# Start addresses of the stationary tiles in a macaron mLSTM and S5 layer on one Trainium2 core

## The chip, the core and the metric

The kernel runs on one core of one Trainium2 chip. The core has a matrix engine (TensorE, in the tables PE, and PEld for its weight loads), a vector engine (DVE), a scalar engine (ACT), a general engine (POOL) and a queue for transfers (SP). The metric is the device time of one execution in microseconds, lower is better. A matmul on TensorE takes two operands from the on-chip memory (SBUF): the stationary one, 128 x 128, which a weight load brings into the array, and the moving one, up to 512 columns, which then streams past it. In this text "spacing" is the time from the start of one matmul to the start of the next.

## What is computed

One decoder layer on 256 tokens of width 2048, all in float32: a SwiGLU block, a mixer with four mLSTM heads beside 64 groups of an S5 state space, and a second SwiGLU block, each behind an RMS norm.

```python
x = x + 0.5 * swiglu(rms_norm(x, ffn1_norm), ffn1_w1, ffn1_w3, ffn1_w2)   # D_FF = 5632
h = rms_norm(x, mix_norm)
proj = h @ w_in                       # q|k, v, o, i, f of the mLSTM, u of the S5 part
hm = rms_norm(mlstm_chunkwise(...)) * sigmoid(o)
y = gelu(real(scan(S5)) + d_skip * u); hs = y * sigmoid(y @ w_glu + b_glu)
x = x + concat(hm, hs) @ w_out
x = x + 0.5 * swiglu(rms_norm(x, ffn2_norm), ffn2_w1, ffn2_w3, ffn2_w2)
out = rms_norm(x, final_norm)
```

## The kernel before

The weights are read from HBM once. `plan` lists all weight steps; each step is two 128-row slices of one matrix and up to 512 columns. `fetch` loads a step into `wraw` over the SP queue (4 buffers), ACT copies it into `whi` (rounded to the matmul's 32-bit format, 3 buffers), and DVE takes the rest, `wlo = wraw - whi` (3 buffers). Activations are split in the same way into a high and a low part, so one product of the reference is three matmuls: high by high, low by high, high by low.

`step_tok` (line 175) is the main loop, for all products whose result lies with tokens on the partitions. The stationary operand is a 128 x 128 block of an activation, the moving one a row of `whi` or `wlo`, 512 columns wide (344 for the third of `w_in` that holds the output gates, OGW). A step is twelve matmuls: for each of the two slices (kk = 0 and 1) and each of two token halves one with the high and one with the low activation against `whi`, then four against `wlo`. Its stationary tiles are, by stage:

- `xh`, `xl` (four tiles each, 128 x 4 x 256): the transposed x, made by `transpose_x`;
- `gh`, `gl`: the gated products of a SwiGLU, made by `split_T`;
- `hmh`, `hml` and `hsh`, `hsl`: the outputs of the mLSTM heads and of the S5 part, before `w_out`.

`gemm_ch` (lines 223, 224, 229) makes the products whose result lies with channels on the partitions (u, q, k, and the S5 gate). There the roles are exchanged: 128-column blocks of `whi` and `wlo` are stationary, and `xh`, `xl` or `yh`, `yl` move, 256 columns at a time. `tail_mm` (lines 477 to 479) makes the last quarter of the last product with 256 moving columns.

Everything on SBUF comes from pools of tiles. The pools lie one behind the other along a partition in the order in which `setup`, `ffn` and `mixer` open them, and the tiles of a pool in the order in which they are first asked for, each rounded up to 32 bytes. So the length of an early tile sets where all later ones begin. In the order of their places: constants, `x`, `xh`/`xl`, `wraw`, `whi`, `wlo`, small tiles, `junk`, the S5 tiles (`s5k0`, `s5rot`, `s5w1`, `s5w2`), and then the pools of a stage, which begin with `gh`/`gl` in the SwiGLU blocks and with `uT`, `u4`, `yT`, `yh`, `yl` and the tiles that `hmh`, `hml`, `hsh`, `hsl` share in the mixer. `WIDE` is the width of the four tiles `qkp0`, `qkp1`, `vx0` and `vx1`; `hmh` and `hml` are put into the same places later.

The order of work on each engine is the program's own, with matters that fill gaps (the S5 parameters in the first block, the S5 groups in the mixer) spread over the weight steps by `tick`. Names on the rows below: `accb` and `tpb` are PSUM banks, `tpb<-ident,s` is a transposition on TensorE of the gated products (the identity moves, `s` is stationary), `tpb<-u,w1x` a product of the S5 part in plain float32, `u<-uT` the transfer that rearranges the S5 input inside SBUF, `s5rot<-spillrot` the load of an S5 table that the first block had written to HBM.

Of the kernel before, what the change touches and what calls it, by code (L numbers as in the profile page):

```python
# [8 lines left out]
F32 = mybir.dt.float32  # L9
F32R = mybir.dt.float32r  # L10
# [6 lines left out]
P = 128  # L17
S = 256
TT = S // P
# [3 lines left out]
NC = 512  # L23
# [12 lines left out]
EPS = 1e-6  # L36
S5_RATE = 0.62
AHEAD = 2
WIDE = 1152
WARM = 7  # L40
MAGIC = 12582912.0
LOG2E = 1.4426950408889634
# [18 lines left out]
class _Layer:  # L61
# [174 lines left out]
    def setup(self):  # L236
        nc = self.nc
        self.const = self.pool("const")
        self.xp = self.pool("xp")
        self.xTp = self.pool("xTp")  # L240
        self.wraw = self.pool("wrawp", 4)
        self.whi = self.pool("whip", 3)
        self.wlo = self.pool("wlop", 3)
        self.small = self.pool("small", 2)
        self.junkp = self.pool("junkp", 1)
        self.s5p = self.pool("s5p", 2)
        self.dram = self.ctx.enter_context(self.tc.tile_pool(name="s5dram", bufs=1, space=DRAM))
        self.acc = self.ctx.enter_context(self.tc.tile_pool(name="acc", bufs=4, space=PSUM))
        self.tp = self.ctx.enter_context(self.tc.tile_pool(name="tp", bufs=4, space=PSUM))
        c = self.const  # L250
        self.x = [self.xp.tile([P, TT, NC], F32, name=f"x{i}") for i in range(4)]
        xin = self.a["x"][0].rearrange("(t p) n -> p t n", p=P)
        vec0 = self.s5p.tile([KD, P], F32, name="vec0", tag="s5k0")
        nc.sync.dma_start(out=vec0, in_=self.a["ffn1_norm"][0].rearrange("(k p) -> k p", p=P))
        self.load_x = lambda i, a=0, b=NC: nc.sync.dma_start(out=self.x[i][:, :, a:b],
                                                             in_=xin[:, :, i * NC + a:i * NC + b])
        idle = self.junkp.tile([P, NC + 112], F32, name="junk")[:, :NC]
        nc.vector.memset(idle, 0.0)
        self.idle = idle.bitcast(mybir.dt.bfloat16)[:, :NC]
        self.warm(WARM)  # L260
        self.ident = c.tile([P, P], F32, name="ident")
        make_identity(nc, self.ident)
        self.ones = c.tile([P, P], F32, name="ones")
        nc.vector.memset(self.ones, 1.0)
        nc.scalar.activation(self.ones[:, 0:1], self.ones[:, 0:1], AF.Square)
        self.mhalf = c.tile([P, 72], F32, name="mhalf")[:, :8]
        nc.vector.memset(self.mhalf, -0.5)
        self.cols0 = c.tile([P, KD], F32, name="cols0")
        b = self.bank()
        nc.tensor.transpose(b[:, :KD], vec0, self.ident[:KD, :KD])  # L270
        nc.vector.tensor_copy(self.cols0, b[:, :KD])
        rows = 16 + 16 + 32 + 8 * 4
        vecs = self.s5p.tile([rows, P], F32, name="vecs", tag="s5k0")
        r = 0
        where = {}
        for name, n in (("mix_norm", 16), ("ffn2_norm", 16), ("conv_w", 32), ("conv_b", 8), ("mlstm_norm", 8),
                        ("d_skip", 8), ("b_glu", 8)):
            src = self.a[name][0]
            if name == "conv_w":
                src = src.rearrange("w (j p) -> (w j) p", p=P)  # L280
            elif name == "d_skip":
                src = src.rearrange("(j r) h -> j (r h)", r=8)
            else:
                src = src.rearrange("(k p) -> k p", p=P)
            nc.gpsimd.dma_start(out=vecs[r:r + n, :], in_=src)
            where[name] = r
            r += n
        self.cols = c.tile([P, rows], F32, name="cols")

        def late():  # L290
            b = self.bank()
            nc.tensor.transpose(b[:, :rows], vecs, self.ident[:rows, :rows])
            nc.vector.tensor_copy(self.cols, b[:, :rows])
            w = where["b_glu"]
            nc.vector.tensor_scalar(self.cols[:, w:w + 8], self.cols[:, w:w + 8], 0.5, None, op0=ALU.mult)
            w = where["mlstm_norm"]
            nc.vector.tensor_scalar(self.cols[:, w:w + 8], self.cols[:, w:w + 8], 0.5, None, op0=ALU.mult)
        self.after(6, late)
        self.col = lambda name, i: self.cols[:, where[name] + i:where[name] + i + 1]
        gb = c.tile([P, 2, H], F32, name="gb")  # L300
        nc.gpsimd.dma_start(out=gb[:, 0, :], in_=self.a["b_i"][0].partition_broadcast(P))
        nc.gpsimd.dma_start(out=gb[:, 1, :], in_=self.a["b_f"][0].partition_broadcast(P))
        self.gb = gb
# [22 lines left out]
    def transpose_x(self, c, gain, halves=(0, 1)):  # L326
        nc = self.nc
        if halves[0] == 0:
            self.xh[c] = self.xTp.tile([P, 4, S], F32R, name=f"xh{c}")
            self.xl[c] = self.xTp.tile([P, 4, S], F32R, name=f"xl{c}")  # L330
        xh, xl = self.xh[c], self.xl[c]
        for half in halves:
            b = self.bank()
            for i in range(2):
                kt = half * 2 + i
                for t in range(TT):
                    o = i * S + t * P
                    nc.tensor.transpose(b[:, o:o + P], self.x[c][:, t, kt * P:(kt + 1) * P], self.ident)  # L338
            for i in range(2):
                kt = half * 2 + i  # L340
                g = gain(c * 4 + kt)
                src = b[:, i * S:(i + 1) * S]
                nc.scalar.activation(xh[:, kt, :], src, AF.Copy, scale=g)
            for i in range(2):
                kt = half * 2 + i
                g = gain(c * 4 + kt)
                src = b[:, i * S:(i + 1) * S]
                nc.vector.scalar_tensor_tensor(xl[:, kt, :], src, g, xh[:, kt, :].bitcast(F32),
                                               op0=ALU.mult, op1=ALU.subtract)
# [417 lines left out]
        self.ffn1_rate = n_tasks / (n_steps - 8)  # L767

    def s5_tiles(self, skip=None):
        return [self.s5p.tile([P, w], F32, name=f"s5{nm}") if i != skip else None for i, (nm, w) in  # L770
                enumerate((("rot", 1024), ("w1", 512), ("w2", 512), ("k0", 128)))]


    def mixer(self, chunk_done):
# [4 lines left out]
        with ExitStack() as ctx:  # L779
# [181 lines left out]
            for hf in range(2):  # L961
                acc = self.pair()
                self.gemm_ch(acc, self.xs, win, KD, QK0 + hf * NC)
                qkp[hf] = ma.tile([P, WIDE], F32, name=f"qkp{hf}", tag=f"qkp{hf}")[:, :4 * (S + 3)].rearrange("p (j s) -> p j s", j=4)
                G.memset(qkp[hf][:, :, 0:3], 0.0)
# [60 lines left out]
            for c in range(2):  # L1026
                v = ma.tile([P, WIDE], F32, name=f"vx{c}", tag=f"vx{c}")[:, :4 * (DV + 1)].rearrange("p (t h d) -> p t h d", t=TT, h=2)
                G.memset(v[:, :, :, DV:], 1.0)
# [201 lines left out]
```

## Time and profile before

| what | value |
|---|---|
| median of three runs | 1861.88 us (1860.5 to 1862.27) |
| the profiled execution | 1860.78 us |
| its span, first to last instruction | 1859.1 us |
| TensorE busy with matmuls | 1826.6 us, 98% of the span |
| DVE, ACT, POOL busy | 1072.0, 817.7, 346.6 us |
| mean granted clock of TensorE | 0.993 of full speed |

The profiled execution took 1.7 us more than its span, and lies 1.1 us under the median. A busy TensorE is not one at its peak: the records of matmuls overlap, since each is drawn with the time that it needs to run through. So the spacing of the starts is what says how fast the stream goes.

### The profile page before, as it was taken

The numbers are of one execution on the slowest core, as the hardware profiler recorded it, in microseconds if no ns is written. First come the engines' busy times: TensorE is split into PE (matmuls) and PEld (weight loads), VectorE is DVE, ScalarE is ACT, GpSimd is POOL, SyncE is SP. The second block draws the span as 40 slices with busy tenths as digits, with TensorE's granted clock in tenths as the row PEclk, the third lists the DMA queues.
The fourth block names the chain that finished last, engine by engine and source line by source line (L and its number), as shares of the span: only waits on it lengthen the run. The fifth ranks groups of instructions, "written<-read, shape, count | busy, mean of one in ns | idle before, by whom it ended". The sixth has DMA issues, their size and how long they took to land.

```text
span 1859.1 us, 24158 instructions
## 1 busy us (share of the span) xinstructions
PE 1826.6 (98%) x9221; PEld 1541.4 (83%) x9221; DVE 1072.0 (58%) x1287; ACT 817.7 (44%) x977; POOL 346.6 (19%) x525
## 2 busy tenths in 40 slices
PE   9999999999999999997999999999999999999998
PEld 7888888888888888986978888888888888888887
DVE  5457866555555555587888765545554444455454
ACT  6444444344444445433544464444443334444443
POOL 3000999900000000175324200000000000000011
PEclk9999999999999999998999999999999999999999
DMA  8666676676666665876766556666665566666554
GB/s 264 192 192 181 194 219 210 220 228 204 191 197 200 185 197 194 206 167 180 156 172 178 177 183 213 191 186 190 190 190 192 194 194 187 191 192 191 188 195 141
DMA packets 191252, 358.27 MB, mean 193 GB/s; under 512 B 12320, under 2 KB 29344, under 8 KB 191008
## 3 DMA queue, kind: packets, MB, share of 16 engines
q1 hardware_dynamic: 186992, 344.58, 63.3%
q0 software_dynamic: 4000, 11.10, 1.6%
q8 instruction: 72, 1.18, 0.3%
q10 hardware_dynamic: 144, 1.05, 0.1%
q14 instruction: 44, 0.36, 0.1%
HBM read 344.62 MB, written 11.01 MB: 191 GB/s over the span
## 4 chain that ended last, share of the span: by engine, by line
PE 93%; DVE 3%; DMA 1%; issue 1%; ACT 0%; POOL 0%; SPq 0%; ACTq 0%; DVEq 0%; POOLq 0%
PE accb L175 83%; PE accb L223 2%; PE accb L224 2%; PE accb L229 2%; DVE wlo L157 1%; PE tpb L489 1%; DMA wraw<-in_w_in_dram 1%; DVE A L869 1%; PE tpb L338 1%; PE tpb L854 0%; PE accb L479 0%; PE accb L478 0%; PE accb L477 0%; DMA u<-uT 0%; PE tpb L893 0%
## 5 line engine op out<-in xcount | busy, mean ns | idle before, releaser
L157 DVE TENSOR_TENSOR wlo<-wraw,whi 128x1024 fp32r<-128x1024 f32 (+1 forms) x630 | 789.9, 1256 | 691.5 <-ACT whi L155 689.3
L155 ACT CAST whi<-wraw 128x1024 fp32r<-128x1024 f32 (+1 forms) x630 | 656.5, 1043 | 926.3 <-PE accb L175 817.5
L175 PE MATMUL accb<-whi,xh 128*128 128x512 f32 (+1 forms) x1568 | 610.1, 389 | 5.9 <-ACT whi L155 5.9
L175 PE MATMUL accb<-whi,xl 128*128 128x512 f32 (+1 forms) x1568 | 605.6, 386 | 0.0
L175 PE MATMUL accb<-wlo,xh 128*128 128x512 f32 (+1 forms) x1568 | 414.7, 386 | 6.8 <-DVE wlo L157 6.8
L175 PEld LDWEIGHTS accb<-whi,xh 128*128 128x128 f32 x1568 | 295.6, 189 | 64.8 <-ACT whi L155 7.2
L175 PEld LDWEIGHTS accb<-wlo,xh 128*128 128x128 f32 x1568 | 293.2, 189 | 66.7 <-DVE wlo L157 8.9
L175 PEld LDWEIGHTS accb<-whi,xl 128*128 128x128 f32 x1568 | 296.0, 189 | 56.5
L175 PE MATMUL accb<-whi,gh 128*128 128x512 f32 x664 | 259.8, 391 | 0.0
L175 PE MATMUL accb<-whi,gl 128*128 128x512 f32 x664 | 258.4, 389 | 0.0
L175 PE MATMUL accb<-wlo,gh 128*128 128x512 f32 x664 | 177.5, 389 | 0.0
L175 PEld LDWEIGHTS accb<-wlo,gh 128*128 128x128 f32 x664 | 124.7, 188 | 25.9
L175 PEld LDWEIGHTS accb<-whi,gh 128*128 128x128 f32 x664 | 124.7, 188 | 25.5
L175 PEld LDWEIGHTS accb<-whi,gl 128*128 128x128 f32 x664 | 124.7, 188 | 25.4
L1194 POOL TENSOR_TENSOR x<-x,fn 128x512 f32<-128x512 f32 x6 | 11.9, 1999 | 689.1 <-ACT junk L320 689.1
L699 POOL TENSOR_TENSOR tr<-s5rot,sp 128x128 f32<-128x128 f32 (+6 forms) x112 | 60.4, 540 | 152.4 <-DVE sp L639 148.9
L223 PE MATMUL accb<-xh,whi 128*128 128x256 f32 x256 | 64.0, 288 | 0.0
L701 POOL TENSOR_TENSOR s5rot<-tr,tr 128x128 f32<-128x128 f32 (+6 forms) x112 | 63.0, 574 | 3.3
L224 PE MATMUL accb<-xl,whi 128*128 128x256 f32 x256 | 63.5, 285 | 0.0
L760 POOL DMA_DIRECT2D spillw<-s5w x16 | 8.7, 543 | 255.1 <-ACT s5w L731 244.7
L700 POOL TENSOR_TENSOR tr<-s5rot,sp 128x128 f32<-128x128 f32 (+6 forms) x112 | 52.2, 467 | 0.0
L223 PEld LDWEIGHTS accb<-xh,whi 128*128 128x128 f32 x256 | 49.4, 193 | 1.0 <-issue 0.9
(313 smaller groups left out, 1346.3 us busy)
## 6 DMA issues: line engine op xcount, KB each, us to landing
wraw<-in_ffn_w_dram SPq DMA_DIRECT2D x528, 512.0 KB, 3.8
wraw<-in_w_in_dram SPq DMA_DIRECT2D x48, 512.0 KB, 5.4
wraw<-in_w_out_dram SPq DMA_DIRECT2D x32, 512.0 KB, 4.3
wraw<-in_w_in_dram SPq DMA_DIRECT2D x24, 344.0 KB, 5.4
spillrot<-s5rot POOLq DMA_DIRECT2D x8, 512.0 KB, 4.6
spillw<-s5w POOLq DMA_DIRECT2D x16, 256.0 KB, 4.4
s5rot<-spillrot SPq DMA_DIRECT2D x8, 512.0 KB, 7.3
wraw<-in_w_glu_dram SPq DMA_DIRECT2D x8, 512.0 KB, 4.2
```

The lines of the kernel that those rows point to most:

```text
L155: nc.scalar.copy(hi, raw)
L157: nc.vector.tensor_sub(lo, raw, hi.bitcast(F32))
L175: nc.tensor.matmul(acc[t][:, :n], lhsT=x, rhs=wt, start=first and t not in seen, stop=last and t not in left)
L223: nc.tensor.matmul(o(nt), lhsT=wh[:, kk, ns(nt)], rhs=xh, start=st, stop=False, **kw)
L224: nc.tensor.matmul(o(nt), lhsT=wh[:, kk, ns(nt)], rhs=xl, start=False, stop=False, **kw)
L229: nc.tensor.matmul(o(nt), lhsT=wl[:, kk, ns(nt)], rhs=xh, start=False, stop=sp, **kw)
L338: nc.tensor.transpose(b[:, o:o + P], self.x[c][:, t, kt * P:(kt + 1) * P], self.ident)
L489: nc.tensor.transpose(b[:, o:o + P], s[t][:, kt * P:(kt + 1) * P], self.ident)
L699: G.tensor_tensor(tr[0][:, :, :k], rv[:, 0, :, 0:k], u0, op=ALU.mult)
L700: G.tensor_tensor(tr[1][:, :, :k], rv[:, 1, :, 0:k], u1, op=ALU.mult)
L701: G.tensor_tensor(rv[:, a, :, k:2 * k], tr[0][:, :, :k], tr[1][:, :, :k], op=op)
L869: V.tensor_tensor_scan(x, Rt[j % 2].rearrange("p q c -> p (q c)"), x, 0.0, op0=ALU.mult, op1=ALU.add)
```

## The change

Four lengths are changed, and with them the places of the tiles behind them. `x3` gets 32 float32 more at its end (128 bytes), so that `xh` and `xl` begin 128 bytes later; `xl3` gets 96 more, so that `wraw`, `whi` and `wlo`, which follow, begin 512 bytes later than before. Each of the two buffers of `s5k0` gets 24 more (96 bytes), so that all that follows moves by 192 bytes beside that. `WIDE` goes from 1152 to 1088 (256 bytes less for each of four tiles).

```diff
-WIDE = 1152
+WIDE = 1088
...
-        self.x = [self.xp.tile([P, TT, NC], F32, name=f"x{i}") for i in range(4)]
+        self.x = [self.xp.tile([P, TT * NC + (32 if i == 3 else 0)], F32, name=f"x{i}")[:, :TT * NC]
+                  .rearrange("p (t n) -> p t n", t=TT) for i in range(4)]
...
-            self.xl[c] = self.xTp.tile([P, 4, S], F32R, name=f"xl{c}")
+            self.xl[c] = (self.xTp.tile([P, 4 * S + (96 if c == 3 else 0)], F32R, name=f"xl{c}")[:, :4 * S]
+                          .rearrange("p (k s) -> p k s", k=4))
...
-        return [self.s5p.tile([P, w], F32, name=f"s5{nm}") if i != skip else None for i, (nm, w) in
+        return [self.s5p.tile([P, w + 24 * (nm == "k0")], F32, name=f"s5{nm}")[:, :w] if i != skip else None for i, (nm, w) in
```

Where the tiles begin, as the number of bytes past a multiple of 512, from the lengths in the order of the pools (the blocks that a matmul takes out of a tile are whole multiples of 512 bytes further on, but for the 344-column steps: their second row begins 344 x 4 = 1376 bytes on, which is 352 past a multiple):

| tiles | before | after |
|---|---|---|
| `whi`, `wlo`, `wraw`, `x` | 0 | 0 |
| `xh`, `xl` | 0 | 128 |
| `gh`, `gl`, `hsh`, `hsl`, `hml`, `yh`, `yl` | 0 | 192 |
| `hmh` | 0 | 448 |
| `uT`, `u4`, `s5rot`, `s5w1`, `s5w2`, `fn`, `s0`, `s1` | 0 | 192 |
| `s5k0`, two buffers | 0, 0 | 0, 96 |
| `ident` (moves in transpositions) | 128 | 128 |
| `w1x`, `qkc`, `A0` to `A3` | 96 | 288 |

No instruction is added, removed, resized or moved: on each of the five queues every row stands in the same order, with the same operands and the same waits. No buffer is added or shared in another way.

## Rows read from the trace of the kernel before

**Rows 1.** The page: engines' busy time, the granted clock, the chain by line.

```profile
span 1859.1 us, 24158 instructions
PE 1826.6 (98%) x9221; PEld 1541.4 (83%) x9221; DVE 1072.0 (58%) x1287; ACT 817.7 (44%) x977; POOL 346.6 (19%) x525
...
PEclk9999999999999999998999999999999999999999
...
PE 93%; DVE 3%; DMA 1%; issue 1%; ACT 0%; POOL 0%; SPq 0%; ACTq 0%; DVEq 0%; POOLq 0%
PE accb L175 83%; PE accb L223 2%; PE accb L224 2%; PE accb L229 2%; DVE wlo L157 1%; PE tpb L489 1%; DMA wraw<-in_w_in_dram 1%; DVE A L869 1%; PE tpb L338 1%; PE tpb L854 0%; PE accb L479 0%; PE accb L478 0%; PE accb L477 0%; DMA u<-uT 0%; PE tpb L893 0%
```

**Rows 2.** Chain in order of time: start us, length us, what and how many instructions.

```profile
755.96 0.96 PE accb L229 x8
...
829.76 10.52 DMA wraw<-in_w_in_dram
...
860.78 5.16 DMA wraw<-in_w_in_dram
...
938.89 1.78 PE tpb L854 x16
...
1393.59 174.10 PE accb L175 x768
1567.69 0.87 PE tpb L489 x8
```

**Rows 3.** Groups by line, shapes apart: count, busy us, mean ns of one, idle before.

```profile
L175 PE MATMUL accb<-whi,xh 128*128 128x512 f32 x1472 | 578.5, 393 | 2.3 <-ACT whi L155 2.3
...
L175 PEld LDWEIGHTS accb<-whi,xh 128*128 128x128 f32 x1568 | 295.6, 189 | 64.8 <-ACT whi L155 7.2 <-issue 0.8
...
L175 PE MATMUL accb<-whi,gh 128*128 128x512 f32 x664 | 259.8, 391 | 0.0
...
L223 PE MATMUL accb<-xh,whi 128*128 128x256 f32 x256 | 64.0, 288 | 0.0
...
L175 PE MATMUL accb<-whi,xh 128*128 128x344 f32 x96 | 31.6, 333 | 3.6 <-ACT whi L155 3.6
...
L175 PE MATMUL accb<-whi,hmh 128*128 128x512 f32 x64 | 25.4, 397 | 0.0
...
L223 PE MATMUL accb<-yh,whi 128*128 128x256 f32 x64 | 15.7, 283 | 0.0
```

**Rows 4.** Timeline of two engines' work in one 512-column step: start us, length us.

```profile
1301.00 0.39 PE L175 MATMUL accb<-whi,xh 128*128 128x512 f32 x1
1301.01 0.19 PEld L175 LDWEIGHTS accb<-whi,xl 128*128 128x128 f32 x1
1301.23 0.39 PE L175 MATMUL accb<-whi,xl 128*128 128x512 f32 x1
...
1301.38 1.23 DVE L157 TENSOR_TENSOR wlo<-wraw,whi 128x1024 fp32r<-128x1024 f32 x1 [0.58 <-ACT whi L155]
1301.45 0.39 PE L175 MATMUL accb<-whi,xh 128*128 128x512 f32 x1
...
1302.36 0.39 PE L175 MATMUL accb<-whi,xh 128*128 128x512 f32 x1
```

**Rows 5.** TensorE's timeline of two 344-column steps, at the full clock.

```profile
811.24 0.32 PE L175 MATMUL accb<-whi,xh 128*128 128x344 f32 x1
...
811.85 0.32 PE L175 MATMUL accb<-whi,xh 128*128 128x344 f32 x1
...
812.48 0.79 PE L175 MATMUL accb<-wlo,xh 128*128 128x344 f32 x4
813.10 0.32 PE L175 MATMUL accb<-whi,xh 128*128 128x344 f32 x1
...
813.74 0.32 PE L175 MATMUL accb<-whi,xh 128*128 128x344 f32 x1
...
814.36 0.79 PE L175 MATMUL accb<-wlo,xh 128*128 128x344 f32 x4
```

**Rows 6.** TensorE's timeline of a 344-column step while half the clock was granted.

```profile
841.87 0.49 PE L175 MATMUL accb<-whi,xl 128*128 128x344 f32 x1
842.15 0.49 PE L175 MATMUL accb<-whi,xh 128*128 128x344 f32 x1
842.44 0.49 PE L175 MATMUL accb<-whi,xl 128*128 128x344 f32 x1
842.73 0.49 PE L175 MATMUL accb<-whi,xh 128*128 128x344 f32 x1
843.01 0.49 PE L175 MATMUL accb<-whi,xl 128*128 128x344 f32 x1
843.30 1.06 PE L175 MATMUL accb<-wlo,xh 128*128 128x344 f32 x3
```

**Rows 7.** Busy time by stretch: us, then PE, PEld, DVE, ACT, POOL, granted clock, DMA.

```profile
815.00:890.00 75.00, 61.12 (x456) 56.21 (x456) 53.96 (x55) 31.48 (x45) 44.90 (x29) 0.93 0.77 178
...
841.45:844.40 2.95, 2.95 (x12) 2.95 (x12) 2.95 (x5) 1.36 (x2) 0.47 (x1) 0.53 0.96 306
...
1393.59:1567.00 173.41, 173.41 (x766) 143.62 (x766) 85.06 (x76) 68.49 (x68) 0.00 (x0) 1.00 0.62 192
```

**Rows 8.** The S5 transfers: times to landing, and who waited for the first.

```profile
L813 POOL DMA_DIRECT2D u<-uT x16: 551/551/599, 780.5 to 812.3; - x16
...
  PE tpb L854: 0.5, 1
...
DMA to landing us min/median/max: 4.5/5.7/7.1
...
L837 SPq DMA_DIRECT2D s5rot<-spillrot x8: 349/460/1513, 771.3 to 999.0; - x8
...
DMA to landing us min/median/max: 3.0/5.6/9.2
```

## The prediction

> **What bounds the kernel now.** I read the page first, then the chain in order of time, then the starts in the timeline. The page puts TensorE on 93% of the chain and line 175 alone on 83% [rows 1]; DVE is busy 58% and ACT 44%, so neither sets the pace outside the mixer. The reader should then look past "busy": what counts is the spacing of matmul starts. The chain holds one unbroken piece of 768 matmuls at line 175 in 174.10 us, which is 226.7 ns each [rows 2]. Single starts say the same: 1301.00, 1301.23, 1301.45, and 1302.36 six matmuls after the first, 0.227 us each [rows 4]. The 256-column matmuls stand 0.96 us / 8 = 120 ns apart [rows 2]. At the 2.4 GHz level, which the granted clock of 1.00 means [rows 7], 512 columns are 213.3 ns and 256 are 106.7 ns. So a matmul costs N / 2.4 + 13.3 ns, with the same 13.3 ns at either width.
>
> How much that is: from the counts by form [rows 3] there are 6792 matmuls of 512 columns (1472 x 3 with x, 664 x 3 with the gated products, 64 x 6 with the two mixer outputs, where a group stands for its like), 288 of 344 (96 x 3), and 1200 of 256 (256 x 3 with x and 64 x 3 with y in the channel products, and 20 slices x 2 token halves x 2 column halves x 3 in the tail). 6792 x 226.7 + 1200 x 120 + 288 x 157 = 1539.7 + 144.0 + 45.2 = 1729 us, 93% of the span. The 13.3 ns are 8280 x 13.3 = 110 us of it. That is all that an address could give back on TensorE; and every nanosecond per matmul is 8.3 us, or 0.45%. A measurement of this kernel can tell about 0.2%, 3.7 us, from no change; that is 0.45 ns per matmul.
>
> **The change, part by part.** Instructions, their order, waits and buffers stay. So there is one term on the path, 8280 matmuls times the change d of the spacing, and a few terms beside it.
>
> *The weight load.* Stationary blocks of x, g and the mixer outputs no longer begin on a 512-byte line, so each block lies across two lines. The load takes 189 ns [rows 3] and begins 0.01 us after the start of the matmul before [rows 4]; the next matmul starts 0.23 us after. It has some 30 ns of cover at 512 columns. In the channel products the stationary operand is a weight block, which stays on its line. So a slower load is hidden until it grows by 30 ns; I put it at nothing. Without that cover each ns would cost 7 us (7080 matmuls of line 175).
>
> *The moving stream.* This is the term that matters: does the read of the moving row lose time to the read of the next stationary block, and does that depend on where each begins? Nothing here has a stationary block off the line in this format, so I bound it by the nearest rows. The 344-column steps have moving rows at 0 (kk = 0) and at 352 bytes (kk = 1), against stationary blocks at 0. If sharing a line start were what costs 13.3 ns, the second four of a step would run faster. They don't [rows 5]: 811.24 to 811.85 and 813.10 to 813.74 are 0.61 and 0.64 us for four with both on the line, mean 156 ns; 811.85 to 812.48 and 813.74 to 814.36 are 0.63 and 0.62 us for four apart by 352 bytes, mean 156 ns. So d = 0 within the reading of the starts, 0.01 us in eight, about 1 ns; I take 0. There is a second reason. DVE and ACT read and write the same memory all the time, DVE 85.1 and ACT 68.5 of 173.4 us [rows 7], a DVE subtraction even starts in the middle of the step of rows 4, and the spacing stays 226.7 ns. A stream that lost time to other readers of the memory would show it there.
>
> The ends of d, both sides: in rows 5 the same step shape runs at 153 ns (0.61 / 4) in one step and at 160 ns (0.64 / 4) in another, with equal start offsets. So the stream can settle 3.4 ns under, or 3.3 ns over, the usual 156.7 (344 / 2.4 + 13.3). Times 8280 that is -28 and +27 us.
>
> *Transfers.* `uT` and `u4` move from 0 to 192, and so do the tables that S5 groups load. The first `u<-uT` is waited for by TensorE for 0.5 us, and lands in 4.5 to 7.1 us, median 5.7 [rows 8]. The nearest bound on a shift is that spread: from -0.5 (the wait is all that can go) to +1.4 us; I take 0.3. The Trainium skill speaks against the change here: in "DMA: Bandwidth & Descriptors", section "How a descriptor splits into AXI transactions", a read that does not begin on a 256-byte boundary is fetched from the boundary below. The runs of `uT` are 512 bytes at 192, so by that 22 beats of 32 bytes go where 16 went, and if all of 5.7 us grew so, the sum would have 2.1 us in place of 0.3 (an estimate from that page); no row has such a read of that tile.
>
> *The rest.* DVE, ACT and POOL read tiles at other offsets in the mixer; all stay on multiples of 32 bytes, as those at 96 do now, and I put them at nothing. In 815 to 890 us, where TensorE is busy 61 of 75 us [rows 7], DVE is on the chain and this cover is missing; there each 1% of DVE's 54 us would be 0.5 us. `wraw`, `whi`, `wlo` and `x` stay on their lines, so the split of the weights on ACT and DVE has no reason to change.
>
> *Sum.* 0 for the stream, 0 for the loads, 0.3 for transfers: 1860.8 + 0.3 = 1861.1 for an execution like the profiled one, and 1.1 more for the median, 1862.2. I say 1862. This case's own range is 1858.5 to 1865.5: 0.3 ns of d either way (2.5 us) and the spread of the runs.
>
> **The rivals.**
>
> *The stream settles at a better phase.* For it: the spacing at 344 columns is not fixed, and 153 ns occurs for four matmuls in a row [rows 5], so the 13.3 ns are not a constant of the engine. Against: at 512 and 256 columns it is one value throughout. 1862 - 28 = 1834 us.
>
> *The excess goes almost wholly.* For it: it is absent where the stream has time to spare. At half the clock (0.53 in the stretch [rows 7]) the 344-column starts stand (843.30 - 841.87) / 5 = 286 ns apart [rows 6], and 344 / 1.2 is 286.7: nothing on top. The transpositions, 128 columns in 0.87 us / 8 = 109 ns [rows 2], are 2 ns over 256 periods of 2.4 GHz. So two reads that meet could be the cause, and moving one away the cure. Against: rows 5, where 352 bytes did not cure it. Down to 2 ns over, 11 ns x 8280 = 91 us: 1771 us. The Trainium skill, "TensorE: Matmul & The Clock Gate", section "Back-to-back issue gap", gives N / 2.4 + 2.5 ns for isolated warm matmuls; the 226.7 ns here are 11 above that, and its rule would give 1862 - 89 = 1773. The trace bears that out for transpositions alone.
>
> *Slower, by the stream.* A block across two lines meets the moving row more often, and the stream settles at the 160 ns kind. The place is every matmul, the price +27 us: 1889 us. It decides from 0.45 ns on. For it: the same jitter as above; against: the same constancy.
>
> *Slower, by the S5 loads.* In the mixer the chain passes through two waits for weights, 10.52 and 5.16 us, behind S5 loads on the SP queue [rows 2], and those loads land in 3.0 to 9.2 us, median 5.6 [rows 8]. If the new offsets put them 3.6 us later (the worst over the median) at both places, it is 7.2 us: 1869 us. It decides from 1.9 us each.
>
> *The change does nothing at all* is the forecast itself, since only addresses differ.
>
> **How the numbers follow.** No change 0.50; better phase 0.19; excess gone 0.09; S5 loads 0.12; worse phase 0.10. The likeliest is 1862. The range goes from 1832, under the better phase, to 1872, over the late loads; it leaves out 0.09 below and 0.10 above. Faster 0.28, same 0.50, slower 0.22.
>
> **What would show it.** In the changed kernel's timeline the starts of 512-column matmuls should stand 226.7 ns apart with x, g and the mixer outputs alike, and those of 256 columns 120 ns. A long piece at line 175 shorter or longer than 174.1 us for 768 decides the matter at once, and if only steps with x, or only those with g, change, the offset of 128 or of 192 is what acts. A longer weight load than 189 ns with equal spacing would show that its cover holds. The first wait at line 854 and the weights' waits at 830 and 861 us show the transfers. The forecast is wrong if the spacing moves by over 0.45 ns.

## The result, and the profile after

The changed kernel takes 1890.39 us (median of 4 runs, 1888.96 to 1892.29) against 1862.08 us for the kernel before on the same chip: a ratio of 1.0154 with a 95% interval of 1.0141 to 1.0166. It is slower by 28 us. The profiled execution took 1890.39 us, with a span of 1888.7 us and a mean granted clock of 0.994 (0.993 before). The forecast was 1862 us. The time that came is that of the rival "slower, by the stream", 1889 us.

The page of the kernel after, its engines' line and its chain by engine and by line, answers to [rows 1]:

```profile
span 1888.7 us, 24158 instructions
...
PE 1855.2 (98%) x9221; PEld 1541.4 (82%) x9221; DVE 1072.8 (57%) x1287; ACT 815.1 (43%) x977; POOL 341.0 (18%) x525
...
PE 93%; DVE 3%; DMA 1%; issue 1%; ACT 0%; POOL 0%; SPq 0%; ACTq 0%; POOLq 0%; DVEq 0%
```

Nothing has changed its place: TensorE is still 93% of the chain, DVE and ACT have the same busy time as before to 0.4%. Only TensorE's own time is longer. The chain of waits in order of time (start us, length us, what, how many instructions) says where; it answers to [rows 2]:

```profile
769.26 0.96 PE accb L229 x8
...
797.71 7.56 DMA u<-uT
...
844.28 9.81 DMA wraw<-in_w_in_dram
...
1189.04 44.62 PE accb L175 x192
...
1416.62 176.76 PE accb L175 x768
1593.38 0.87 PE tpb L491 x8
```

The piece of 768 matmuls grew from 174.10 to 176.76 us. The pieces of 192 are steps with x alone: 44.62 / 192 = 232.4 ns each, where 226.7 stood before. The piece of 768 holds 192 matmuls with x and 576 with gated products, so the latter stand (176.76 - 44.62) / 576 = 229.4 ns apart. The 256-column products at line 229 and the transpositions (line 491 now, 489 before) have the times that they had, 0.96 and 0.87 us for eight.

TensorE's timeline of one step with x in the kernel after (start us, length us), beside [rows 4]:

```profile
1319.84 0.40 PE L175 MATMUL accb<-whi,xh 128*128 128x512 f32 x1
1320.07 0.40 PE L175 MATMUL accb<-whi,xl 128*128 128x512 f32 x1
...
1320.77 1.09 PE L175 MATMUL accb<-wlo,xh 128*128 128x512 f32 x4
1321.69 0.40 PE L175 MATMUL accb<-whi,xh 128*128 128x512 f32 x1
1321.94 0.40 PE L175 MATMUL accb<-whi,xl 128*128 128x512 f32 x1
...
1322.63 0.39 PE L175 MATMUL accb<-whi,xh 128*128 128x512 f32 x1
```

Twelve matmuls take 1322.63 - 1319.84 = 2.79 us, 232.5 ns each, and no longer at an even pace: the one from 1321.69 to 1321.94 takes 0.25 us. The weight loads have not grown. Two groups by form of the kernel after (count, busy us, mean ns of one, idle before), against [rows 3]:

```profile
L175 PEld LDWEIGHTS accb<-whi,xh 128*128 128x128 f32 x1568 | 296.1, 189 | 72.2 <-ACT whi L155 6.6 <-issue 0.8 <-ACT xh L345 0.2
...
L175 PEld LDWEIGHTS accb<-whi,gh 128*128 128x128 f32 x664 | 124.8, 188 | 27.1
```

From here on "spacing of a kind" is the mean over the whole trace of the differences between the start of a matmul and the start of the next, with differences over 16 ns above the median left out, since there a wait lies between. With x and 512 columns it went from 226.9 to 232.7 ns, with g from 226.8 to 229.2, with the mixer outputs from 227.2 to 229.2; with 344 columns from 156.8 to 157.2. With 256 columns it fell: 119.9 to 119.4 with x, 120.0 to 117.8 with y, 120.0 to 114.7 in the tail. Times the counts: 4416 x 5.8 + 1992 x 2.4 + 384 x 2.0 - 240 x 5.3 - 192 x 2.2 - 768 x 0.5 = 25.6 + 4.8 + 0.8 - 1.3 - 0.4 - 0.4 = 29.1 us. The span grew by 1888.7 - 1859.1 = 29.6 us. The spacing accounts for the result; what remained is why it moved. (What the span holds beside this stream, 140.5 us in the kernel before, varies from 138.4 to 144.4 us in the traces of the other kernels below, so some 2 to 4 us of a comparison need not be the stream's.)

### The profile page after: what moved, and what is told of

The parts are those of the page before. It is cut to its first block, busy times and chain, and to the rows that moved or that the text cites. A ratio compares the mean times of both kernels' runs of the same rounds, so it can differ in the third digit from the quotient of the medians.

```text
span 1888.7 us, 24158 instructions
## 1 busy us (share of the span) xinstructions
PE 1855.2 (98%) x9221; PEld 1541.4 (82%) x9221; DVE 1072.8 (57%) x1287; ACT 815.1 (43%) x977; POOL 341.0 (18%) x525
## 4 chain that ended last, share of the span: by engine, by line
PE 93%; DVE 3%; DMA 1%; issue 1%; ACT 0%; POOL 0%; SPq 0%; ACTq 0%; POOLq 0%; DVEq 0%
PE accb L175 84%; PE accb L224 2%; PE accb L223 2%; PE accb L229 2%; DVE wlo L157 1%; PE tpb L491 1%; PE tpb L856 1%; DVE A L871 1%; DMA wraw<-in_w_in_dram 1%; PE tpb L340 0%; DMA wraw<-in_ffn_w_dram 0%; DMA u<-uT 0%; PE tpb L895 0%; PE accb L481 0%; PE accb L480 0%
## 5 line engine op out<-in xcount | busy, mean ns | idle before, releaser
L175 PE MATMUL accb<-whi,xh 128*128 128x512 f32 (+1 forms) x1568 | 618.0, 394 | 5.3 <-ACT whi L155 5.3
L175 PE MATMUL accb<-whi,xl 128*128 128x512 f32 (+1 forms) x1568 | 612.5, 391 | 0.8 <-DVE xl L350 0.8
L175 PE MATMUL accb<-wlo,xh 128*128 128x512 f32 (+1 forms) x1568 | 423.2, 391 | 8.1 <-DVE wlo L157 8.1
L703 POOL TENSOR_TENSOR s5rot<-tr,tr 128x128 f32<-128x128 f32 (+6 forms) x112 | 56.7, 518 | 3.3
```

The source lines that it names most:

```text
L175: nc.tensor.matmul(acc[t][:, :n], lhsT=x, rhs=wt, start=first and t not in seen, stop=last and t not in left)
L703: G.tensor_tensor(rv[:, a, :, k:2 * k], tr[0][:, :, :k], tr[1][:, :, :k], op=op)
```

## The experiments

All times are medians against the kernel before on the same chip. In what follows, the *distance* is the start of the stationary block less the start of the moving row, modulo 512 bytes: 0 in the kernel before (160 for the second row of the 344-column steps), 128 with x and 192 with g in the kernel after. The first theory is that this distance sets the spacing. The second is that a stationary block that lies across a 512-byte line costs time, whatever the moving row does, which is how the prediction's rival had put it.

### The two parts alone, and all three moved together

`e1_x128` moves x alone; g and the mixer outputs stay on a line, and `WIDE` is 1088 as in the change.

```diff
-WIDE = 1152
+WIDE = 1088
-        self.x = [self.xp.tile([P, TT, NC], F32, name=f"x{i}") for i in range(4)]
+        self.x = [self.xp.tile([P, TT * NC + (32 if i == 3 else 0)], F32, name=f"x{i}")[:, :TT * NC]
+                  .rearrange("p (t n) -> p t n", t=TT) for i in range(4)]
-            self.xl[c] = self.xTp.tile([P, 4, S], F32R, name=f"xl{c}")
+            self.xl[c] = (self.xTp.tile([P, 4 * S + (96 if c == 3 else 0)], F32R, name=f"xl{c}")[:, :4 * S]
+                          .rearrange("p (k s) -> p k s", k=4))
```

> xh and xl begin 128 bytes past a line, everything else on it (the four tiles of WIDE are 1088 wide, so hmh begins at 256). Both theories, distance between the two operands and crossing of a line by the stationary block, expect the 512-column matmuls with x as in the changed kernel, 232.6 ns mean, and those with the gated products as before, 226.7 ns. 4416 matmuls x 5.8 ns = 26 us: 1887 to 1888 us. If the two offsets act on each other, the time is not the sum.

Measured: 1884.63 us, ratio 1.0121 (1.0106 to 1.0136). `e2_g192` moves g, the mixer outputs and the S5 tiles alone, by a longer `junk`:

```diff
-WIDE = 1152
+WIDE = 1088
-        idle = self.junkp.tile([P, NC + 112], F32, name="junk")[:, :NC]
+        idle = self.junkp.tile([P, NC + 160], F32, name="junk")[:, :NC]
```

> Only the tiles behind the small ones move: gh, gl, hsh, hsl, hml, yh, yl and the S5 tiles begin 192 bytes past a line, xh, xl, whi, wlo on it. Both theories expect 229.1 ns for the gated products (1992 matmuls x 2.4 ns = 4.8 us) and the mixer outputs (384 x 2.4 = 0.9 us), less 1 to 2 us in the tail and the S5 gate, and 226.7 ns with x: 1865 to 1868 us. If the S5 transfers of the mixer were to blame for part of the loss, it shows here as more than that.

Measured: 1864.46 us, ratio 1.0015 (1.0005 to 1.0024). The two parts, 22.9 and 2.8 us, make 25.7 of the 28.3 us; `e1_x128` came about 3 us under its expectation though its spacings with x are those of the kernel after (232.7 ns), and what its span holds beside the stream is 2.1 us shorter than before. `e3_all128` moves x by 128 bytes and lets all that lies behind follow, so that x, the weights and g all begin 128 bytes past a line. Every stationary block then lies across two lines, and every distance is 0 (256 for `hmh`, which `WIDE` moves).

```diff
-WIDE = 1152
+WIDE = 1088
-        self.x = [self.xp.tile([P, TT, NC], F32, name=f"x{i}") for i in range(4)]
+        self.x = [self.xp.tile([P, TT * NC + (32 if i == 3 else 0)], F32, name=f"x{i}")[:, :TT * NC]
+                  .rearrange("p (t n) -> p t n", t=TT) for i in range(4)]
```

> Everything that TensorE reads in the large products begins 128 bytes past a line: stationary and moving tiles alike. Theory 1, the distance between the starts of the two operands counts: distance 0 as before, 226.7 ns at 512 columns, 1862 us. Theory 2, a stationary block that lies across two lines costs extra: 232.6 ns with x and as much with g, 6792 x 5.8 = 39 us more, 1901 us.

Measured: 1862.72 us, ratio 1.0006 (0.9997 to 1.0016), no change. `e4_w128` does the reverse: x, g and the mixer outputs but `hmh` stay on their lines, and only `wraw`, `whi` and `wlo` move by 128 bytes (distance 384).

```diff
-WIDE = 1152
+WIDE = 1088
-        idle = self.junkp.tile([P, NC + 112], F32, name="junk")[:, :NC]
+        idle = self.junkp.tile([P, NC + 208], F32, name="junk")[:, :NC]
-            self.xl[c] = self.xTp.tile([P, 4, S], F32R, name=f"xl{c}")
+            self.xl[c] = (self.xTp.tile([P, 4 * S + (32 if c == 3 else 0)], F32R, name=f"xl{c}")[:, :4 * S]
+                          .rearrange("p (k s) -> p k s", k=4))
```

> Only the weights, whi and wlo, begin 128 bytes past a line; all activations stay on it. Theory 1, the distance counts: it is 384 (or -128) for every token product, the spacing leaves 226.7 ns for all 6792 matmuls; if the sign doesn't count it is 232.6 ns and 1901 us. Theory 2, crossing by the stationary block: 226.7 ns with x and g, 1862 us, and only the channel products, whose stationary block is a weight, change (960 matmuls, at most 5 us).

Measured: 1897.61 us, ratio 1.0193 (1.0177 to 1.0208). In the chains, the long piece and a piece with x alone, first of `e1_x128`:

```profile
1137.91 44.62 PE accb L175 x192
...
1411.27 175.34 PE accb L175 x768
```

of `e2_g192`:

```profile
1396.59 175.35 PE accb L175 x768
...
1706.08 43.60 PE accb L175 x192
```

of `e3_all128`:

```profile
1397.58 174.13 PE accb L175 x768
...
1705.86 43.57 PE accb L175 x192
```

and of `e4_w128`:

```profile
1422.31 178.47 PE accb L175 x768
...
1738.11 44.62 PE accb L175 x192
```

The reader is to see four things. Moving x alone gives the 44.62 us of the kernel after, and leaves (175.34 - 44.62) / 576 = 226.9 ns for g. Moving g alone gives (175.35 - 43.60) / 576 = 228.7 ns for g, and leaves x at 227.1. With all three moved the times are those of the kernel before, 174.13 and 43.57 us, although every stationary block lies across a line: the second theory falls. With the weights alone moved, x and g alike stand at 232.4 ns ((178.47 - 44.62) / 576), although their blocks lie on their lines. So it is the distance, and 384 costs what 128 costs.

### How the loss goes with the distance

Three more runs change distances only, by the lengths of `x3`, `xl3`, `junk` and `WIDE`. `e5_x32_g64` has x at 32 and g at 64 bytes:

```diff
+        self.x = [self.xp.tile([P, TT * NC + (8 if i == 3 else 0)], F32, name=f"x{i}")[:, :TT * NC]
...
+        idle = self.junkp.tile([P, NC + 128], F32, name="junk")[:, :NC]
...
+            self.xl[c] = (self.xTp.tile([P, 4 * S + (120 if c == 3 else 0)], F32R, name=f"xl{c}")[:, :4 * S]
```

> Two distances in one run: x 32 bytes from the line on which the weights begin, the gated products and S5 outputs 64. So far the distance modulo 256 decides: 0 and 256 give 226.9 to 227.7 ns, 192 and 448 give 229.0, 128 and 384 give 232.5. If the loss grows with the distance from the nearest multiple of 256, 64 gives 229 and 32 about 228: 4416 x 1.1 + 2376 x 2.3 = 10 us, 1872 us. If what counts is only whether the two starts fall on the same 64 bytes, 64 gives 229 to 232 and 32 gives 226.7.

Measured: 1900.96 us, ratio 1.021 (1.0166 to 1.0254), far over the expectation. `e6_x96_g160` has x at 96 and g at 160 (24, 152 and 104 in place of 8, 128 and 120):

```diff
+        self.x = [self.xp.tile([P, TT * NC + (24 if i == 3 else 0)], F32, name=f"x{i}")[:, :TT * NC]
...
+        idle = self.junkp.tile([P, NC + 152], F32, name="junk")[:, :NC]
...
+            self.xl[c] = (self.xTp.tile([P, 4 * S + (104 if c == 3 else 0)], F32R, name=f"xl{c}")[:, :4 * S]
```

> Distances 96 (x) and 160 (g). If the loss grows with the distance from the nearest multiple of 256, both are 96 from it and give 230 to 232 ns, 6792 x 4.5 = 30 us, 1890 us. If each distance has a value of its own, one of them can lie under 226.7.

Measured: 1908.26 us, ratio 1.0249 (1.0205 to 1.0293), the slowest of all. `e7_x224_g256` has x at 224 and g at 256 (56, 176 and 72):

```diff
+        self.x = [self.xp.tile([P, TT * NC + (56 if i == 3 else 0)], F32, name=f"x{i}")[:, :TT * NC]
...
+        idle = self.junkp.tile([P, NC + 176], F32, name="junk")[:, :NC]
...
+            self.xl[c] = (self.xTp.tile([P, 4 * S + (72 if c == 3 else 0)], F32R, name=f"xl{c}")[:, :4 * S]
```

> Distances 224 (x) and 256 (g, hsh, hsl, hml). With a period of 256 bytes the gated products stand 226.7 to 227 ns apart, as the high mLSTM outputs at 256 did (227.3 to 227.7 in 124 matmuls); with a period of 512 they do not. 224 is 32 from a multiple and gives about 228 like 32: 4416 x 1.1 = 5 us, 1867 us.

Measured: 1888.04 us, ratio 1.014 (1.0097 to 1.0184). The same two pieces of the chain, of `e5_x32_g64`:

```profile
1192.40 44.80 PE accb L175 x192
...
1420.78 179.20 PE accb L175 x768
```

of `e6_x96_g160`:

```profile
1198.62 44.98 PE accb L175 x192
...
1427.85 179.41 PE accb L175 x768
```

and of `e7_x224_g256`:

```profile
1185.85 44.79 PE accb L175 x192
...
1414.03 175.54 PE accb L175 x768
```

At 32 bytes x already stands at 44.80 / 192 = 233.3 ns. The loss does not grow with the distance; the expectation that a small distance costs little was wrong. And at 256 bytes g stands at (175.54 - 44.79) / 576 = 227.0 ns, as at 0: the distance counts modulo 256.

Two runs give each of the six tiles that hold a part of the gated products a distance of its own, so that 24 matmuls in a row have the same one, and leave x at 0. `e9_g_sweep1`:

```diff
-                    gh = gp.tile([P, 4, S], F32R, name="gh")
-                    gl = gp.tile([P, 4, S], F32R, name="gl")
+                    oh, ol = [(16, 16), (48, 48), (80, 80), (112, 112), (144, 144), (176, 176)][c]
+                    gh = gp.tile([P, 4 * S + 128], F32R, name="gh")[:, oh // 4:oh // 4 + 4 * S].rearrange(
+                        "p (k s) -> p k s", k=4)
+                    gl = gp.tile([P, 4 * S + 128], F32R, name="gl")[:, ol // 4:ol // 4 + 4 * S].rearrange(
+                        "p (k s) -> p k s", k=4)
```

> Each of the six g tiles of a half begins at a distance of its own inside a wider tile: 16, 48, 80, 112, 144, 176 bytes past the line; 24 matmuls in a row go at one distance, the rest is as before. Measured so far, modulo 256: 0 gives 226.8, 192 gives 229.0, 128 gives 232.5, all other multiples of 32 give 233 to 234. If the line of 256 bytes is all that counts, all six give 229 to 235 and the sum is 1992 x 6 = 12 us more, 1874 us. If there is a finer step (16 or 64 bytes), some of them come back to 226.7 or lower, and the kernel is then to be had faster with it.

Measured: 1873.89 us in one execution, beside 1862.78 of the kernel before. In `e10_g_sweep2` the list is another:

```diff
+                    oh, ol = [(208, 208), (240, 240), (4, 4), (8, 8), (272, 272), (0, 0)][c]
```

> As the run before with distances 208, 240, 4, 8, 272 and 0. Distance 0 is the control: 226.7 ns. 272 and 16 of the other run should agree if the period is 256 bytes. If a distance under 16 bytes is as good as 0, 4 and 8 give 226.7; if the start must be the same to the byte, they give 229 or more. In sum 1868 to 1874 us.

Measured: 1868.79 us in one execution. TensorE's timeline of `e10_g_sweep2`, the first matmul of each 24, in the order of the list and the next round's first:

```profile
1425.85 0.40 PE L175 MATMUL accb<-whi,gh 128*128 128x512 f32 x1
...
1431.41 0.40 PE L175 MATMUL accb<-whi,gh 128*128 128x512 f32 x1
...
1436.88 0.39 PE L175 MATMUL accb<-whi,gh 128*128 128x512 f32 x1
...
1442.46 0.39 PE L175 MATMUL accb<-whi,gh 128*128 128x512 f32 x1
...
1447.99 0.40 PE L175 MATMUL accb<-whi,gh 128*128 128x512 f32 x1
...
1453.59 0.39 PE L175 MATMUL accb<-whi,gh 128*128 128x512 f32 x1
...
1459.06 0.40 PE L175 MATMUL accb<-whi,gh 128*128 128x512 f32 x1
```

The 24 take 5.56 us at 208, 5.47 at 240, 5.58 at 4, 5.53 at 8, 5.60 at 272 and 5.47 at 0. One float32 of distance, 4 bytes, costs here as much as 128 bytes. The mean over all such stretches of 24 in both kernels, and the spacings of the runs before, worked out from the starts in ns:

```
distance  spacing      distance  spacing      distance  spacing
     0     226.8          64      233.3         176      230.4
     4     232.3          80      232.0         192      229.1
     8     230.6          96      234.2         208      232.0
    16     231.2         112      233.3         224      233.3
    32     233.3         128      232.7         240      228.1
    48     233.3         144      233.2         256      226.8
                         160      233.3         272      233.3
                                                384      232.5
```

0 and 256 agree, and so do 128 and 384: the period of 256 bytes holds. Inside it there is no slope but a floor at 0, a level of about 233.3, and some values between.

The 231.2 at 16 is a mean of two paces. TensorE's timeline of `e9_g_sweep1` shows the first of twelve matmuls and the first of the next twelve, all at a distance of 16: first behind a stretch at 176, then behind steps with x at 0:

```profile
350.26 0.40 PE L175 MATMUL accb<-whi,gh 128*128 128x512 f32 x1
...
353.06 0.40 PE L175 MATMUL accb<-whi,gh 128*128 128x512 f32 x1
...
1395.17 0.39 PE L175 MATMUL accb<-whi,gh 128*128 128x512 f32 x1
...
1397.89 0.39 PE L175 MATMUL accb<-whi,gh 128*128 128x512 f32 x1
```

Twelve take 2.80 us, 233.3 ns each, or 2.72 us, 226.7 ns each. All four stretches at 16 that follow x keep the even pace of 226 and 227 ns to their end; of the eleven that follow an uneven stretch, nine stay at about 233.3, as 272 does, and two take up the even pace behind a pause. At 0, where the stretches of `e10_g_sweep2` follow uneven ones at 272, and at 240 the stream finds the even pace by itself: in 8 of 8 and 12 of 15 stretches all but some first matmuls stand at 226 or 227. So the distance alone does not set the spacing; near a multiple of 256 the pace that the stream comes with counts too. The stretches at 4 follow those at 240, most of them in the even pace, and lose it; 4 bytes right behind a stream at 0 were not tried.

### What the load has to do with it

`e8_half_load` keeps every distance at 0, and gives the matmuls of the low weights only 64 stationary columns, so that each of their loads reads half. It leaves out half of the output rows of those products.

```diff
+            m = 64 if len(left) < len(late) else P
-            nc.tensor.matmul(acc[t][:, :n], lhsT=x, rhs=wt, start=first and t not in seen,
-                             stop=last and t not in left)
+            nc.tensor.matmul(acc[t][:m, :n], lhsT=x[:, :m], rhs=wt, start=first and t not in seen,
+                             stop=last and t not in left, skip_group_check=True)
```

> Left out: the matmuls against the low part of the weights in the token products use only 64 of their 128 stationary columns, so their weight loads read 256 bytes per partition in place of 512, and their products for the other 64 tokens are missing. All places are as before. If the 13.3 ns over N / 2.4 come from the read of the next stationary block, the four spacings of a step in which such a half block is loaded fall to about 220 ns and the other eight stay at 226.7: 566 steps x 4 x 6.7 = 15 us less, 1847 us. If they are a fixed price of a matmul, all stay at 226.7 and 1862 us.

Measured: 1878.33 us, ratio 1.0089 (1.0066 to 1.0112): with less work, slower. The group of the half loads by form (count, busy us, mean ns of one, idle before) of `e8_half_load`:

```profile
L176 PEld LDWEIGHTS accb<-wlo,xh 128*64 128x64 f32 x1568 | 209.7, 134 | 132.3 <-DVE wlo L157 10.5 <-issue 0.6
```

and a piece of its chain:

```profile
1179.97 44.07 PE accb L176 x192
```

The half loads are shorter, 134 for 189 ns, yet the mean spacing of the piece is 44.07 / 192 = 229.5 ns, up from 226.7. Had the stream lost time in proportion to what the loads read, it would have gained; had the loads nothing to do with the stream, it would have stayed. Neither of the two expectations came. But a matmul with 64 stationary columns also gives only half of the output rows, so this run does not tell whether the shorter loads disturb the stream or the halved products do. That the load takes part is an inference from the runs that move g alone (`e2_g192`, `e9_g_sweep1`, `e10_g_sweep2`): the place of a stationary block acts, and on TensorE it is the load that reads it.

`e11_g_pairs` gives `gh` and `gl` different distances (the diff is that of `e9_g_sweep1` with another list):

```diff
+                    oh, ol = [(0, 128), (128, 0), (0, 64), (0, 256), (128, 256), (128, 384)][c]
```

> gh and gl at different distances, six pairs: (0,128), (128,0), (0,64), (0,256), (128,256), (128,384). While a product with gh streams against the high weights, the next block to be loaded is gl, and the other way round. If the distance of the block that is being loaded while the row streams counts, pair (0,128) has its long spacing (232) behind the matmuls with gh and 226.7 behind those with gl; if the block already in the array counts, it is the other way round. If the stream keeps a state over several matmuls, both are long and the four against the low weights (gh alone) come back to 226.7 one by one. (0,256) gives 226.7 throughout, (128,384) 232.5, with a period of 256. In sum 1868 to 1872 us.

Measured: 1869.32 us in one execution, beside 1862.78. TensorE's timeline of `e11_g_pairs`: two steps of twelve with (0, 64), from 1437.18, then two with (0, 256), from 1442.70:

```profile
1437.18 0.39 PE L175 MATMUL accb<-whi,gh 128*128 128x512 f32 x1
...
1439.04 1.07 PE L175 MATMUL accb<-wlo,gh 128*128 128x512 f32 x4
1439.95 0.39 PE L175 MATMUL accb<-whi,gh 128*128 128x512 f32 x1
...
1442.70 0.39 PE L175 MATMUL accb<-whi,gh 128*128 128x512 f32 x1
...
1448.15 0.40 PE L175 MATMUL accb<-whi,gh 128*128 128x512 f32 x1
```

The 24 with (0, 256) take 5.45 us, 227.1 ns each: mixing two distances does no harm where both are 0 modulo 256. In the first of the steps with (0, 64) the eight that alternate between `gh` and `gl` take 1.86 us, 232.5 ns each, and the four that follow with `gh` alone, distance 0, 0.91 us, 227.5 each. With (0, 128) the loss lasts longer: over all such steps the eight stand at 232.6 ns, and the four with distance 0 behind them still at 230.0. With (128, 256) the mean is 232.6, and with (128, 384) 233.1, where 232.5 had been expected. So a matmul's pace depends also on those before it. The trace of the kernel before shows the same where all distances are 0: behind 56 pauses the spacing begins at 231.9 ns in the mean, and is 226.9 at the seventh matmul.

### A version that uses it

At 256 columns the runs had shown the opposite sign: in `e2_g192` the products with y, at a distance of 320, stood 113.4 ns apart against 120.0, and the tail 113.3. `e12_apart256` keeps 0 or 256 for 512 columns, and shifts `whi` and `wlo` inside longer tiles by 64 or 128 bytes, so that the steps of the channel products and of the tail come out at 64 or 192 modulo 256 (but for 96 of the 240 in the tail, whose weights lie in the places of `xh` and `xl`: 256). `self.turn` counts the weight steps, since the three buffers take their turns.

```diff
+        oh, ol = self.places(name in ("w_glu",) or name == "w_in" and (c0 >= U0 or c0 < V0))
-        hi = self.whi.tile([P, KK * NC], F32R, name="whi")[:, :kk * n]
+        hi = self.whi.tile([P, KK * NC + 32], F32R, name="whi")[:, oh:oh + kk * n]
-        lo = self.wlo.tile([P, KK * NC], F32R, name="wlo")[:, :kk * n]
+        lo = self.wlo.tile([P, KK * NC + 32], F32R, name="wlo")[:, ol:ol + kk * n]
...
+    def places(self, apart):
+        i = self.turn % 3
+        self.turn += 1
+        return (16, 16) if apart else ((0, 0, 32)[i], (32, 32, 0)[i])
```

> The kernel before with one difference by width: where 256 columns move (the channel products for u, q, k and the S5 gate, and the weights of the tail) whi and wlo begin 64 bytes into their tile, so that the distance of the two operands is 64 or 192 modulo 256; where 512 columns move it stays 0 (the tiles of whi and wlo are 128 bytes longer, and two of three buffers begin with an offset that brings them back to 0). 512 columns at 226.7 ns and distance 0 as before. For 256 columns the runs gave 113.4 to 117.8 ns at distances 64 and 192, against 120.0 at 0: 960 + 144 matmuls x 2.2 to 6.6 ns = 2.4 to 7.3 us less, 1855 to 1860 us. If the distance only ever costs, it is 1862 us or more.

Measured: 1857.61 us (median of 11) against 1861.65 us (median of 15), ratio 0.9977 (0.9968 to 0.9986): faster than both kernels, by 4 us against the one before. Its chain:

```profile
755.84 0.94 PE accb L236 x8
...
1055.37 0.91 PE accb L236 x8
...
1391.62 174.10 PE accb L182 x768
```

The 512-column stream keeps its 174.10 us, and eight 256-column matmuls take 0.91 to 0.94 us where [rows 2] had 0.96. By the spacings it should give 768 x 5.1 (x, 114.8 ns) + 192 x 5.7 (y, 114.3) + 240 x 1.6 (tail, 118.4) = 3.9 + 1.1 + 0.4 = 5.4 us; 4.0 came, and the rest is within what varies beside the stream.

## Why the prediction was wrong

**What failed: "d = 0" in "The moving stream".** The forecast had one term on the path, the matmuls times the change d of the spacing, and put d at 0. It measured +5.8 ns with x and +2.4 with g, 29 us in all. Both reasons for the 0 were misread.

The first was [rows 5]: 344-column steps have moving rows 0 and 352 bytes on (distances 0 and 160), and the mean spacing was the same. That is still so: 156.8 before, 157.2 after, 158.2 in `e6_x96_g160`. But these rows do not stand for 512 columns. At 344 the pace is uneven at distance 0 already, 153 to 160 ns in [rows 5], while at 512 with x it was 226 or 227 in 95% of the differences in the whole trace. There the steady pace was what could be lost, and 344 columns never have it. The narrower width was the nearest row in form and the wrong one in behaviour; a row that lacks the property in question can't show what its loss costs. Better rows lay in the same trace. TensorE's timeline of the kernel before, behind a pause:

```profile
337.18 0.39 PE L175 MATMUL accb<-whi,gl 128*128 128x512 f32 x1
...
338.34 0.39 PE L175 MATMUL accb<-whi,gh 128*128 128x512 f32 x1
...
339.70 0.39 PE L175 MATMUL accb<-whi,gh 128*128 128x512 f32 x1
...
340.38 0.39 PE L175 MATMUL accb<-whi,gl 128*128 128x512 f32 x1
```

Five spacings take 1.16 us, 232 ns each; a little later three take 0.68 us, 227 each. So "at 512 and 256 columns it is one value throughout", which the prediction held against both phase rivals, was not so: 512 columns had a slower pace already, and it is close to the one that came.

The second was that the spacing holds while DVE and ACT read and write the same memory [rows 7]. True, and no evidence on the question: what acts is the place of TensorE's own two operands to each other. The stream of `e3_all128` and that of `e4_w128` have the same loads and the same rows, and differ by 5.6 ns through their relative place alone. In "Step-by-step: what each phase is for", the Trainium skill's "TensorE: Matmul & The Clock Gate" gives the moving operand and the weight load a read port each, and says that loading the next tile takes no read bandwidth from the running matmul. `e3_all128` against `e4_w128`, 1862.72 and 1897.61 us, speaks against that here: the spacing depends on where the two lie to each other.

**The rival that came.** "Slower, by the stream" was priced at 3.3 ns x 8280 = 27 us from the 160 ns kind of [rows 5], and 28 us came. The price fits by some luck: it is 5.8 and 2.4 ns at 512 columns, and below nothing at 256. The mechanism given for it, a block across two lines, is refuted by `e3_all128`, and by the g of `e7_x224_g256`, which begins in the middle of a line and runs at 227.0 ns.

**The range.** The 13.3 ns over N / 2.4 in both widths was taken for one quantity that an address could only give back. The range went to 1872 for late loads, with the worse phase left outside at 0.10. With [rows 5] showing both ends, 153 and 160, there was no reason to give the better phase twice the chance of the worse. At 512 columns no run had a mean spacing under 226.7; at 256 columns 113.4 was seen. The rival "the excess goes" also leaned on the transpositions' 109 ns, which it set against 256 periods. They move 128 columns, which are 53.3 ns at 2.4 GHz, and no row shows that each takes two periods; so no row of the kernel before shows a stream free of the excess at the full clock, and what the prediction says the trace bears out for the transpositions has no row behind it.

**What held.** The loads did not grow, 189 and 188 ns, so their cover was not tried. The waits of the transfers were a small term: TensorE's first wait for `u` went from 0.5 to 1.7 us, inside the bound of +1.4 for the shift, though over the 0.3 taken. That rise can't be put to the places of the tiles: the first transfer is on the chain with 6.37 us before and 7.56 after, but with 6.43 (`e1_x128`) to 7.29 (`e11_g_pairs`) where `uT` stayed on its line. The landing of the sixteen `u<-uT`, at TensorE's later line 856 in the kernel after:

```profile
  PE tpb L856: 1.7, 1
...
DMA to landing us min/median/max: 3.6/5.4/7.7
```

against 4.5, 5.7 and 7.1 in [rows 8]. The median did not lengthen; the 22 beats for 16 that the prediction had worked out from the Trainium skill's "DMA: Bandwidth & Descriptors", "How a descriptor splits into AXI transactions", do not show in it. The loads of weights on the chain at 844 us, 9.81 us, are not longer than the 10.52 of [rows 2]. The eight S5 tables landed in a median of 6.3 us for 5.6, and 8.9 at most for 9.2: the rival "slower, by the S5 loads" did not come.

**What stays open.** Why a 512-column stream finds its even pace at 0 modulo 256 and not at most other distances, and why 256 columns prefer others. That a state is carried over several matmuls is shown by `e11_g_pairs` and by the two paces at a distance of 16; how the two operands' reads meet inside TensorE no trace here shows. At 256 columns the distance alone does not settle the pace either: with y it was 320 in both `e2_g192` and the kernel after, and the spacing 113.4 in one and 117.8 in the other.

## What to carry to other kernels

Where a weight load goes with each matmul of 512 32-bit columns, let the stationary blocks and the moving rows begin at the same place modulo 256 bytes; where on a line both begin did not matter (0 or 128 bytes past it), and padding ahead of one of them can cost 2%, one float32 of it 5.5 of 226.8 ns in the stretches tried. Read the spacing of starts, for each width by itself, before and after any change of tile lengths: TensorE's busy share, 98% in both kernels, and the load durations showed nothing here, and 344 and 256 columns told nothing of 512. A row that is near in form bounds a cost only if it has the property that the change may take away.

## What had not been expected of the hardware

- The spacing of 512-column matmuls depends on the distance between two operands, between 226.8 ns (0 and 256 bytes) and 234.2 ns (96 bytes); at 4 bytes it was 232.3.
- At a distance of 16 bytes the stream has two paces, 226.7 and 233.3 ns, by what ran before it.
- At 256 columns the even pace of 120.0 ns at distance 0 is the slow one; 113.4 ns was seen with y in `e2_g192`.
- Halving the stationary columns of a third of the matmuls (loads of 134 for 189 ns, half the output rows) raised the mean spacing from 226.7 to 229.5 ns.
